# The first four contraction chunks of x and weights loaded one by one, at the start of a decoder layer

## The chip, the cores and the metric

The kernel runs on one core of one Trainium2 chip. The metric is the device time of one execution in microseconds (us), lower is better; a kernel's time is the median of its runs. A profile is one further execution, recorded by the hardware profiler. The engines are TensorE (PE, with its weight loads PEld), VectorE (DVE), ScalarE (ACT), GpSimd (POOL) and SyncE (SP), which only issues loads and stores.

## The reference

One decoder layer for 320 rows: a prompt of 256 and 8 samples of 8. D is 2048, float32 everywhere.

```python
xn = rms_norm(x, g_mix)
z = xn @ w_in                     # B, C, h, q, k, v, gate_conv, gate_attn
u = c_gate * h_conv
y_conv = (b_gate * short_conv(u)) @ w_conv_out
y_attn = window_attention(q, k, v, rel_bias, sinks) @ w_attn_out
m = sigmoid(gate_c) * y_conv + sigmoid(gate_a) * y_attn
h = x + m @ w_o
hn = rms_norm(h, g_ffn)
h = h + (silu(hn @ w_gate) * (hn @ w_up)) @ w_down
y = rms_norm(h, g_final)
```

The new keys and values and the convolution's last rows are outputs too.

## The kernel before

Activations lie with the features on the 128 partitions: x is 16 contraction chunks (KC) of 128 features by 320 rows (T). One chunk of x is 128 x 320 float32, 160 KB. The weights come as float32, too, and every product is made from high and low parts: a raw weight tile `wraw` is cast to `whi` on ScalarE (the cast rounds it to the matmul's input format), DVE subtracts to get the rest, `wlo`, and x is split into `xh_t` and `xl_t` in the same way. Three matmuls are then made for each chunk and column block: high by high, high weights by low x, low weights by high x.

The change touches the first product, the one for keys and values (`kv_product`). Its weights `w_kv` are 512 columns wide, so one chunk is 256 KB and takes 4 column blocks x 3 = 12 matmuls. A list of tile sizes (`tiles`) says how many chunks one weight load brings: 1, 1 and then seven times 2. `load_kv` issues a load, takes a tile for each part, and issues cast and subtraction; raw tiles have four buffers, the parts three each, so that a later load on the SP queue waits for the subtraction that frees its buffer. The first load goes out on ScalarE's queue, all others on SP's.

x comes through the tensor `xv`, whose first 72 columns (VW) are four small vectors (`g_mix`, `g_ffn`, the convolution's weights `wcv`, `g_fin`). It is loaded in pieces of `XB` chunks by `x_load`; the argument `x_after` says behind which weight load each piece is issued on SP. `x_prep` splits a chunk of x: the high part on ScalarE (chunk 0 on DVE), the low part on DVE. Inside the product it is called for the chunks of the next weight tile, behind one of the current tile's matmuls. `tick` takes the next step of `start_rest`: the squares for the norm, and the small loads on POOL, held by `gate` until chunk 3 of x is split.

The order on each engine is that in which the scheduler of the tile framework puts the instructions of the program; it is fixed when the kernel is built, and each engine then works in order.

Ahead of the product PE runs 20 matmuls on a constant tile `busy` (`wm`, L269), whose output is not used; DVE fills the tile first. `first_root` is a square root on ScalarE whose output is not used either; it makes the engine load that function's table.

Of the kernel before, what the change touches and what calls it, by code (L numbers as in the profile page):

```python
# [8 lines left out]
F32 = mybir.dt.float32  # L9
F32R = mybir.dt.float32r  # L10
AF = mybir.ActivationFunctionType
# [6 lines left out]
T = TP + NB * TS  # L18
# [8 lines left out]
P = 128  # L27
KC = D // P
CW = 256
# [2 lines left out]
O_GC = O_Q + NH * HD  # L32
O_GA = O_GC + D
EL = 384
LAG = 3
VW = 72
E0 = D - 512
TR = T - P
XB = [1, 1, 2, 2, 2, 2, 2, 4]
TOK = [(0, 128), (128, 128), (256, 64)]  # L40


# [1 line left out]
def hybrid_layer(ctx: ExitStack, tc: tile.TileContext, a: dict, o: list):  # L44
    nc = tc.nc
    y_0, y_r, nk_p, nv_p, nk_s, nv_s, ncv = o

    w_in, w_kv, w_co, w_ao, w_o, w_g, w_u, w_d = (
        a[n] for n in ("w_in", "w_kv", "w_conv_out", "w_attn_out", "w_o", "w_gate", "w_up", "w_down")
    )  # L50

    cst = ctx.enter_context(tc.tile_pool(name="cst", bufs=1))
# [10 lines left out]
    def ps_aux(name):  # L63
        return aux[0].tile([P, 512], F32, tag="aux", name=name)
# [3 lines left out]
    def u(s):  # L68
        uid[0] += 1
        return f"{s}_{uid[0]}"  # L70

    def after(*marks):

        es = ExitStack()
        for m in marks:
            es.enter_context(tc.issue_after(m.ins))
        return es
# [15 lines left out]
    def split_to(hi, lo, src):  # L93
        last["hi"] = nc.scalar.activation(hi, src, AF.Copy)  # L94
        last["lo"] = nc.vector.tensor_sub(lo, src, hi.bitcast(F32))  # L95
# [12 lines left out]
    last = {}  # L108
# [6 lines left out]
    def passes(order, end):  # L115

        seq, low = [], []
        for k, c in order:
# [3 lines left out]
            low.append((k, c, 2))  # L122
            if len(low) > LAG:
                seq.append(low.pop(0))
# [43 lines left out]


    ident = cst.tile([P, P], F32, name="ident")  # L170
    busy = cst.tile([P, CW], mybir.dt.bfloat16, name="busy")
    busy_in = nc.vector.memset(busy, 1.0)
    ones = cst.tile([P, 1], F32, name="ones")
    ones_r = cst.tile([P, P], F32R, name="ones_r")
    with after(busy_in):
        nc.vector.memset(ones, 1.0)
        nc.vector.tensor_copy(ones_r, ones.to_broadcast([P, P]))
    st_sb = cst.tile([P, 8, 2 * NB], F32, name="st_sb")
    sink_bc = cst.tile([P, NH], F32, name="sink_bc")
    nsink = cst.tile([P, NH], F32, name="nsink")  # L180
# [36 lines left out]
    xp = ctx.enter_context(tc.tile_pool(name="xp", bufs=1))  # L217
    xh_t = xp.tile([P, KC, T], F32R, tag="xh", name="xh_t")
    xl_t = xp.tile([P, KC, T], F32R, tag="xl", name="xl_t")

    xv = xp.tile([P, VW + KC * T], F32, name="xv")
    g_mix, g_ffn, wcv, g_fin = xv[:, 0:16], xv[:, 16:32], xv[:, 32:56], xv[:, 56:VW]
    hT = xv[:, VW:].rearrange("p (k t) -> p k t", k=KC)
    e_scr = dr.tile([NH, EL], F32, name="e_scr")

    def xh(kc):
# [18 lines left out]
    oh_r = zz.tile([NBK, WIN], F32R, name="oh_r")  # L245
    e_sb = zz.tile([NH, EL], F32, name="e_sb")

# [2 lines left out]
    st = sp.enter_context(tc.tile_pool(name="st", bufs=1))  # L250

    def x_load(i):
        c0, c1 = (VW + sum(XB[:j]) * T if j else 0 for j in (i, i + 1))
        nc.sync.dma_start(xv[:, c0:c1], a["x_v"][:, c0:c1])

    x_load(0)
    x_load(1)

    first_root = st.tile([P, 1], F32, name="first_root")
    nc.scalar.activation(first_root, ones, AF.Sqrt)  # L260
    nc.gpsimd.memset(ident, 0.0)
    nc.gpsimd.affine_select(
        out=ident, in_=ident, compare_op=ALU.not_equal, fill=1.0, base=0, pattern=[[-1, P]],
# [1 line left out]
    )  # L265

    wm = ps_aux("wm")
    for n in [CW] * 13 + [P] * 7:
        nc.tensor.matmul(wm[:, :n], busy[:, :P], busy[:, :n], start=True, stop=True)  # L269

    def x_prep(kc):
        if kc == 0:
            m1 = nc.vector.tensor_scalar(xh_t[:, kc, :], hT[:, kc, :], g_mix[:, kc:kc + 1], None, op0=ALU.mult)
        else:
            m1 = nc.scalar.activation(xh_t[:, kc, :], hT[:, kc, :], AF.Copy, scale=g_mix[:, kc:kc + 1])
        m2 = nc.vector.scalar_tensor_tensor(
            xl_t[:, kc, :], hT[:, kc, :], g_mix[:, kc:kc + 1], xh_t[:, kc, :].bitcast(F32),
            op0=ALU.mult, op1=ALU.subtract,
        )
        mark[kc] = (m1, m2)  # L280

    CK = 2 * DKV

    def load_kv(k0, n):
        raw = wp.tile([P, KT // 2, CK], F32, tag="wraw", name=u("wraw"), bufs=4)
        (nc.scalar if k0 == 0 else nc.sync).dma_start(raw[:, :n, :], w_kv[0, :, k0:k0 + n, :])
        hi = wp.tile([P, KT // 2, CK], F32R, tag="whi", name=u("whi"), bufs=3)
        lo = wp.tile([P, KT // 2, CK], F32R, tag="wlo", name=u("wlo"), bufs=3)
        with after(*mark[k0]):
            if k0 == 0:  # L290
                nc.scalar.activation(hi[:, 0, :CW], raw[:, 0, :CW], AF.Copy)
                last["hi"] = nc.scalar.activation(hi[:, 0, CW:], raw[:, 0, CW:], AF.Copy)
                last["lo"] = nc.vector.tensor_sub(lo[:, 0, :], raw[:, 0, :], hi[:, 0, :].bitcast(F32))
            else:
                split_to(hi[:, :n, :], lo[:, :n, :], raw[:, :n, :])
        return hi, lo

    def kv_product(tiles, x_after):

        ps = [ps_acc(u("kv")) for _ in range(4)]  # L300
        k0 = 0
        x_prep(0)
        for i, n in enumerate(tiles):
            hi, lo = load_kv(k0, n)
            if i == 0:
                x_prep(1)
            for b in x_after.get(i, ()):
                x_load(b)
            order = [(k, c) for k in range(n) for c in range(4)]
            if k0 + n == KC:  # L310
                order.sort(key=lambda kc: kc[1])
            seq = passes(order, k0 + n == KC)
            if i == 0:
                seq.sort(key=lambda kcm: kcm[2])
            for k, c, m in seq:
                kc = k0 + k
                if k0 and (k, c, m) == (0, 3 if n > 1 else 1, 0) and k0 + n < KC:
                    x_prep(k0 + n)
                    x_prep(k0 + n + 1)
                    tick()  # L320
                w, x = ((hi, xh), (hi, xl), (lo, xh))[m]
                last["mm"] = nc.tensor.matmul(  # L322
                    ps[c][:, :T], w[:, k, c * P:(c + 1) * P], x(kc),
                    start=(kc == 0 and m == 0), stop=(kc == KC - 1 and m == 2),
                )
            k0 += n
            if i == 0:
                tick()
        return ps
# [4 lines left out]
    def small_loads():  # L334

        behind = nc.gpsimd.tensor_copy(gate, xh_t[:, 3, 0:1].bitcast(F32))
        with after(behind):
            nc.gpsimd.dma_start(rel, a["rel_bias"])
            nc.gpsimd.dma_start(oh, a["c_onehot"])
            nc.gpsimd.dma_start(sink_bc, sk[0].partition_broadcast(P))  # L340
            nc.gpsimd.dma_start(sink_s, bass.AP(sk.tensor, sk.offset, [[1, NH], [0, TS], [1, 1]]))
            nc.gpsimd.dma_start(st_sb, a["state_t"])
            nc.gpsimd.dma_start(blk, a["c_block"])

    def squares(*chunks):

        for k in chunks:
            t = tmp("t" + "abcd"[k % 4], "sq")[:, :T] if k else xacc
            nc.scalar.activation(t, hT[:, k, :], AF.Square)
            if k:  # L350
                nc.vector.tensor_add(xacc, xacc, t)

    def start_rest():
        squares(0)
        yield
        small_loads()
        squares(1)
        for k in range(2, 12, 2):
            yield
            squares(k, k + 1)  # L360

    side_work[0] = start_rest()
    ps_kv = kv_product([1, 1] + [2] * 7, {1: (2,), 2: (3,), 3: (4,), 4: (5, 6), 5: (7,)})
    for _ in side_work[0]:
        pass
    for c in range(2):
# [11 lines left out]
    def first_norm():  # L378
# [15 lines left out]
        for z in (vT, kT):  # L394
# [5 lines left out]
        nc.gpsimd.dma_start(  # L400
            bias_s, bass.AP(e_scr.tensor, e_scr.offset + WIN - TS, [[EL, NH], [1, TS], [1, WIN + TS]])
        )
# [56 lines left out]
    def bias_load(kv, gp):  # L459
# [3 lines left out]
            bass.AP(  # L463
                e_scr.tensor, e_scr.offset + (kv * GRP + gp * 2) * EL, [[1, P], [EL, 2], [1, 2 * WIN]]
            ),
# [260 lines left out]
    for cp in range(4):  # L726
        c_sb = []
        ps = in_pair(O_C + cp * CW, "C")
        for c in range(2):
            t = tmp("ta", "csb")  # L730
# [4 lines left out]
        for c in range(2):  # L735
# [13 lines left out]
            n = UL - 2  # L749
# [11 lines left out]
        for c in range(2):  # L761
            ch = cp * 2 + c
            cv, cs = conv[c]
            t = tmp("td", "bc")
# [24 lines left out]
    for mp in range(8):  # L789
        c0 = mp * CW  # L790
        sg = {}
        for nm, off, tag in (("gc", O_GC, "ta"), ("ga", O_GA, "tb")):
            ps = in_pair(off + c0, nm)
            for c in range(2):
                t = tmp(tag, nm)[:, :T]
# [12 lines left out]
        for c in range(2):  # L808
            t = sg["ga", c]
# [11 lines left out]
    for mp in range(8):  # L821
        c0 = mp * CW
# [4 lines left out]
        for c in range(2):  # L827
            k = mp * 2 + c
# [8 lines left out]
            else:  # L837
                t = tmp("tc", "sq")[:, :T]
# [66 lines left out]
    for half in range(2):  # L905
# [5 lines left out]
        for fpair in range(nf // 2):  # L911
            c0 = (f0 + fpair * 2) * P
# [9 lines left out]
            for c in range(2):  # L922
                t, t2 = tmp("ta", "gs")[:, :T], tmp("tb", "sg")[:, :T]
# [76 lines left out]
    for j in range(nf // 2):  # L1000
        raw = wp.tile([P, 2, 512], F32, tag="wraw", name=u("wraw"), bufs=4)
        nc.sync.dma_start(raw, w_d[E0 // 512, :, FH[0] + 2 * j:FH[0] + 2 * j + 2, :])
        if j < 5:
            src, n = (free, 2 * j) if j < 3 else (more, 2 * (j - 3))
            hi, lo = (
                src[:, i * KT * CW:(i + 1) * KT * CW].rearrange("p (k n) -> p k n", k=2) for i in (n, n + 1)
            )
        else:
            hi = wp.tile([P, 2, 512], F32R, tag="whi", name=u("whi"), bufs=3)
# [28 lines left out]
    for c in range(4):  # L1038
        k = E0 // P + c
# [12 lines left out]
    for c in (2, 3):  # L1052
        k = E0 // P + c
# [126 lines left out]
```

## Time and profile before

| | |
|---|---|
| runs | 1678.95, 1676.19, 1676.61 us; median 1676.61 |
| profiled execution | 1676.44 us, its span 1674.5 us |
| mean granted TensorE clock | 0.998 |
| TensorE busy | 1664.1 us, 99% |
| DVE busy | 893.3 us, 53% |
| ACT busy | 651.1 us, 39% |
| read from HBM | 253.30 MB, 154 GB/s over the span |

The span goes from the first to the last recorded instruction; the rest of the execution's time lies around it. The rows of a timeline give start and duration in us, engine, line, operation, what is written and read, how many instructions were merged, and in brackets how long the engine was idle before and what ended that. In a table of stages the columns are the stage, its length, the busy time of PE, PEld, DVE, ACT and POOL with instruction counts, the granted clock, the DMA engines' mean busy share, and GB/s. Matmuls overlap: a duration is longer than the distance to the next start.

### The profile page before, as it was taken

Reading aid. Unit: us, or ns where it says so; the run is one execution under the profiler, and the core shown is the slowest. Engines: PE = TensorE matmul, PEld = TensorE weight load, DVE = VectorE, ACT = ScalarE, POOL = GpSimd, SP = SyncE. Lnnn points to the kernel's source line nnn. Section 1 sums busy time; section 2 is a strip of 40 time slices with the busy share of each in tenths; the row PEclk is TensorE's granted clock in tenths of the full one; section 3 lists DMA queues with packets and bytes.
Section 4 is the critical chain, followed back from the end, with each engine's and each line's share of the span. In section 5 each row is a group of like instructions: output and inputs, shape, how many; then the busy total and the mean of one; then the engine's idle time right before and its main releaser. Section 6 shows DMA issues by size and latency. Waiting matters only on the chain.

```text
span 1674.5 us, 26375 instructions
## 1 busy us (share of the span) xinstructions
PE 1664.1 (99%) x10983; PEld 1621.4 (97%) x10983; DVE 893.3 (53%) x1298; ACT 651.1 (39%) x863; POOL 79.5 (5%) x120
## 2 busy tenths in 40 slices
PE   9999999999999999999999999999999999999997
PEld 9999999999999999999999999998888999999887
DVE  7779554444444445556555555553444455555556
ACT  6445433333333333334333333333333333334443
POOL 0111311000000002320000000000000000000000
PEclk9999999999999999999999999999999999999999
DMA  7554546544444444444444444445555444444552
GB/s 257 169 153 140 177 138 185 160 150 150 150 152 151 151 149 150 148 149 149 151 151 151 151 150 148 148 149 151 150 151 151 151 151 151 151 151 149 175 167 89
DMA packets 73391, 258.13 MB, mean 154 GB/s; under 512 B 8440, under 2 KB 10920, under 8 KB 73144
## 3 DMA queue, kind: packets, MB, share of 16 engines
q1 hardware_dynamic: 71160, 250.28, 48.2%
q0 software_dynamic: 1968, 5.90, 1.3%
q8 instruction: 86, 1.41, 0.3%
q14 instruction: 33, 0.27, 0.0%
q10 hardware_dynamic: 144, 0.26, 0.0%
HBM read 253.30 MB, written 5.08 MB: 154 GB/s over the span
## 4 chain that ended last, share of the span: by engine, by line
PE 99%; DVE 0%; DMA 0%; SPq 0%; ACT 0%; issue 0%; DVEq 0%
PE fg L141 18%; PE fu L141 18%; PE dn L879 9%; PE ga L141 7%; PE wo L141 7%; PE gc L141 7%; PE dn L887 6%; PE B L141 3%; PE q L141 3%; PE C L141 3%; PE yc L141 3%; PE H L141 3%; PE ya L141 3%; PE dl L883 2%; PE kv L322 1%; PE dn L1026 1%
## 5 line engine op out<-in xcount | busy, mean ns | idle before, releaser
L95 DVE TENSOR_TENSOR wlo<-wraw,whi 128x1024 fp32r<-128x1024 f32 (+1 forms) x459 | 561.5, 1224 | 637.1 <-ACT whi L94 629.4
L94 ACT ACTIVATE whi<-wraw 128x1024 fp32r<-128x1024 f32 (+1 forms) x459 | 485.5, 1059 | 779.8 <-PE dn L879 157.7
L879 PE MATMUL dn<-a_t,whi 128*128 128x512 f32 x640 | 218.8, 394 | 0.0
L141 PE MATMUL fg<-hh_t,whi 128*128 128x320 f32 x704 | 212.4, 309 | 0.0
L141 PE MATMUL fu<-hh_t,whi 128*128 128x320 f32 x704 | 212.4, 309 | 0.0
L141 PE MATMUL fg<-hl_t,whi 128*128 128x320 f32 x704 | 212.3, 309 | 0.0
L141 PE MATMUL fu<-hl_t,whi 128*128 128x320 f32 x704 | 212.3, 309 | 0.0
L141 PE MATMUL fg<-hh_t,wlo 128*128 128x320 f32 x704 | 164.0, 309 | 0.0
L141 PE MATMUL fu<-hh_t,wlo 128*128 128x320 f32 x704 | 164.0, 309 | 0.0
L887 PE MATMUL dn<-a_t,wlo 128*128 128x320 f32 x640 | 152.0, 309 | 0.0
L879 PEld LDWEIGHTS dn<-a_t,whi 128*128 128x128 f32 x640 | 119.2, 188 | 23.5
L141 PEld LDWEIGHTS fg<-hl_t,whi 128*128 128x128 f32 x704 | 132.1, 188 | 0.0
L141 PEld LDWEIGHTS fu<-hl_t,whi 128*128 128x128 f32 x704 | 132.1, 188 | 0.0
L141 PEld LDWEIGHTS fg<-hh_t,whi 128*128 128x128 f32 x704 | 132.1, 188 | 0.0
L141 PEld LDWEIGHTS fu<-hh_t,whi 128*128 128x128 f32 x704 | 132.1, 188 | 0.0
L887 PEld LDWEIGHTS dn<-a_t,wlo 128*128 128x128 f32 x640 | 112.4, 188 | 10.9
L141 PEld LDWEIGHTS fu<-hh_t,wlo 128*128 128x128 f32 x704 | 118.5, 188 | 0.0
L141 PEld LDWEIGHTS fg<-hh_t,wlo 128*128 128x128 f32 x704 | 118.5, 188 | 0.0
L141 PE MATMUL ga<-xh_t,whi 128*128 128x320 f32 x256 | 77.3, 310 | 0.0
L141 PE MATMUL gc<-xh_t,whi 128*128 128x320 f32 x256 | 77.3, 310 | 0.0
L141 PE MATMUL ga<-xl_t,whi 128*128 128x320 f32 x256 | 77.3, 310 | 0.0
L141 PE MATMUL gc<-xl_t,whi 128*128 128x320 f32 x256 | 77.3, 310 | 0.0
(311 smaller groups left out, 2749.1 us busy)
## 6 DMA issues: line engine op xcount, KB each, us to landing
wraw<-in_w_in_dram SPq DMA_DIRECT2D x128, 512.0 KB, 3.8
wraw<-in_w_gate_dram SPq DMA_DIRECT2D x88, 512.0 KB, 3.8
wraw<-in_w_up_dram SPq DMA_DIRECT2D x88, 512.0 KB, 3.8
wraw<-in_w_down_dram SPq DMA_DIRECT2D x88, 512.0 KB, 3.7
wraw<-in_w_o_dram SPq DMA_DIRECT2D x32, 512.0 KB, 3.8
wraw<-in_w_conv_out_dram SPq DMA_DIRECT2D x16, 512.0 KB, 3.7
wraw<-in_w_attn_out_dram SPq DMA_DIRECT2D x16, 512.0 KB, 3.7
wraw<-in_w_kv_dram SPq DMA_DIRECT2D x7, 512.0 KB, 7.6
```

The lines of the kernel that those rows point to most:

```text
L94: last["hi"] = nc.scalar.activation(hi, src, AF.Copy)
L95: last["lo"] = nc.vector.tensor_sub(lo, src, hi.bitcast(F32))
L141: last["mm"] = nc.tensor.matmul(ps[c][:, :T], w[:, k, c * P:(c + 1) * P], x(kc), start=(kc == 0 and i == 0), stop=(kc == nk - 1 and i == 2),)
L322: last["mm"] = nc.tensor.matmul(ps[c][:, :T], w[:, k, c * P:(c + 1) * P], x(kc), start=(kc == 0 and m == 0), stop=(kc == KC - 1 and m == 2),)
L879: nc.tensor.matmul(ps[c], parts[k][0][:, cs], a_t[:, k, 0:512], start=k == 0, stop=False)
L883: nc.tensor.matmul(low, a_t[:, k, 512:], parts[k][0], start=k == 0, stop=k == nf - 1 and c0 < E0)
L887: last["mm"] = nc.tensor.matmul(ps[c][:, :T], parts[k][1][:, cs], a_t[:, k, 0:T], start=False, stop=k == nf - 1)
L1026: nc.tensor.matmul(ps[c][:, P:512], held[k][0][:, cs], a_t[:, k, P:512], start=k == 0, stop=k == nf - 1)
```

## The change

The first four chunks of x and of the `w_kv` weights are loaded and split one by one: `tiles` becomes four times 1 and six times 2, `XB` 1, 1, 1, 1, 2, 2, 2, 2, 4, and the pieces 7 and 8 are both issued behind the weight load of tile 5. The very first weight load becomes two, of 256 columns each, and its cast three, of 128, 128 and 256 columns. The square root on ScalarE is issued behind these loads. Of the small vectors only `g_mix` stays ahead of x; the others move to the end of the tensor and come with its last piece, and `xv` keeps its size. The warm-up reads a bf16 constant that the preamble has written, in place of `busy`, and has 15 matmuls of 256 columns and 7 of 128 instead of 13 and 7.

```diff
+VX = 16 + KC * T
-VW = 72
+VW = 16
-XB = [1, 1, 2, 2, 2, 2, 2, 4]
+XB = [1, 1, 1, 1, 2, 2, 2, 2, 4]
...
-    busy = cst.tile([P, CW], mybir.dt.bfloat16, name="busy")
-    busy_in = nc.vector.memset(busy, 1.0)
     ones = cst.tile([P, 1], F32, name="ones")
     ones_r = cst.tile([P, P], F32R, name="ones_r")
-    with after(busy_in):
-        nc.vector.memset(ones, 1.0)
-        nc.vector.tensor_copy(ones_r, ones.to_broadcast([P, P]))
+    nc.vector.memset(ones, 1.0)
+    nc.vector.tensor_copy(ones_r, ones.to_broadcast([P, P]))
...
-    xv = xp.tile([P, VW + KC * T], F32, name="xv")
-    g_mix, g_ffn, wcv, g_fin = xv[:, 0:16], xv[:, 16:32], xv[:, 32:56], xv[:, 56:VW]
-    hT = xv[:, VW:].rearrange("p (k t) -> p k t", k=KC)
+    xv = xp.tile([P, VX + 56], F32, name="xv")
+    g_mix, g_ffn, wcv, g_fin = xv[:, 0:VW], xv[:, VX:VX + 16], xv[:, VX + 16:VX + 40], xv[:, VX + 40:]
+    hT = xv[:, VW:VX].rearrange("p (k t) -> p k t", k=KC)
...
     def x_load(i):
-        c0, c1 = (VW + sum(XB[:j]) * T if j else 0 for j in (i, i + 1))
+        c0, c1 = (VW + sum(XB[:j]) * T if 0 < j < len(XB) else j and VX + 56 for j in (i, i + 1))
         nc.sync.dma_start(xv[:, c0:c1], a["x_v"][:, c0:c1])
...
-    nc.scalar.activation(first_root, ones, AF.Sqrt)
...
     wm = ps_aux("wm")
-    for n in [CW] * 13 + [P] * 7:
-        nc.tensor.matmul(wm[:, :n], busy[:, :P], busy[:, :n], start=True, stop=True)
+    one = lambda n: nc.const_aps.tensor(1.0, [P, n], mybir.dt.bfloat16)
+    for n in [CW] * 15 + [P] * 7:
+        nc.tensor.matmul(wm[:, :n], one(P), one(n), start=True, stop=True)
...
     def load_kv(k0, n):
         raw = wp.tile([P, KT // 2, CK], F32, tag="wraw", name=u("wraw"), bufs=4)
-        (nc.scalar if k0 == 0 else nc.sync).dma_start(raw[:, :n, :], w_kv[0, :, k0:k0 + n, :])
+        if k0 == 0:
+            for c0 in (0, CW):
+                behind = nc.scalar.dma_start(raw[:, 0, c0:c0 + CW], w_kv[0, :, 0, c0:c0 + CW])
+
+            with after(behind):
+                nc.scalar.activation(first_root, ones, AF.Sqrt)
+        else:
+            nc.sync.dma_start(raw[:, :n, :], w_kv[0, :, k0:k0 + n, :])
...
             if k0 == 0:
-                nc.scalar.activation(hi[:, 0, :CW], raw[:, 0, :CW], AF.Copy)
-                last["hi"] = nc.scalar.activation(hi[:, 0, CW:], raw[:, 0, CW:], AF.Copy)
+                for c0, c1 in ((0, P), (P, CW), (CW, CK)):
+                    last["hi"] = nc.scalar.activation(hi[:, 0, c0:c1], raw[:, 0, c0:c1], AF.Copy)
...
                 if k0 and (k, c, m) == (0, 3 if n > 1 else 1, 0) and k0 + n < KC:
-                    x_prep(k0 + n)
-                    x_prep(k0 + n + 1)
+                    for kk in range(tiles[i + 1]):
+                        x_prep(k0 + n + kk)
                     tick()
...
     def start_rest():
         squares(0)
         yield
+        squares(1)
+        yield
         small_loads()
-        squares(1)
-        for k in range(2, 12, 2):
+        squares(2)
+        yield
+        squares(3)
+        for k in range(4, 12, 2):
             yield
             squares(k, k + 1)
...
-    ps_kv = kv_product([1, 1] + [2] * 7, {1: (2,), 2: (3,), 3: (4,), 4: (5, 6), 5: (7,)})
+    ps_kv = kv_product([1] * 4 + [2] * 6, {1: (2,), 2: (3,), 3: (4,), 4: (5, 6), 5: (7, 8)})
...
-    inputs["x_v"] = _np.concatenate([vec.T, by_feature(x).reshape(P, -1)], axis=1)
+    inputs["x_v"] = _np.concatenate([vec.T[:, :16], by_feature(x).reshape(P, -1), vec.T[:, 16:]], axis=1)
```

In the changed kernel, the instructions stand on the two queues in this order, from the end of the single chunks to the weights of chunks 8 and 9:

```
SP:   weights 4,5 | x 6,7 | x 8,9 | weights 6,7 | x 10,11 | x 12 to 15 and vectors | weights 8,9
ACT:  cast weights 6,7 | squares 6, 7 | x splits 10, 11 | x splits 12, 13, 14, 15 | cast weights 8,9
```

In the kernel before, the weights of chunks 8 and 9 stand behind x 10,11 and ahead of x 12 to 15 on both.

## Prediction

> **What bounds the kernel now.** I read the page first, then the chain of waits over the first 40 us, the timeline of the start, the landing times of the single loads, and the page's queues last. The page says that TensorE (PE) is the bound nearly throughout.
>
> ```profile
> span 1674.5 us, 26375 instructions
> ## 1 busy us (share of the span) xinstructions
> PE 1664.1 (99%) x10983; PEld 1621.4 (97%) x10983; DVE 893.3 (53%) x1298; ACT 651.1 (39%) x863; POOL 79.5 (5%) x120
> ```
>
> PE is not busy for 1674.5 - 1664.1 = 10.4 us in all. No edit in the first stage can be worth more than that, and every edit here acts in the first stage. After it PE runs on without a break, so a microsecond won or lost at the start arrives at the end whole. The profiled execution took 1676.44 us, 1.94 us more than its span and 0.17 us below the median of the three runs (1676.61); I work against the profiled one. Here is what holds the start (chain of waits, first 40 us; start, duration, what):
>
> ```profile
> 2.60 6.13 DMA wraw<-in_w_kv_dram
> ...
> 8.76 1.07 ACT whi L94
> ...
> 9.87 25.08 PE kv L322 x168
> 34.95 5.13 PE q L141 x35
> ```
>
> The third weight load, a pair of contraction chunks (2 and 3), lands at 8.73; ScalarE needs 1.07 us to cast it; then PE works without a break until the next product. So before 9.87 transfers set the pace, and from there PE does. The timeline shows how the first product begins:
>
> ```profile
> 0.86 0.27 DVE L172 MEMSET busy<- 128x256 bf16 x1 [0.86 <-PEq L1163]
> ...
> 1.18 1.28 ACT L260 ACT_TABLE_LOAD   x1 [1.18 <-PEq L1163]
> ...
> 1.19 3.70 PE L269 MATMUL wm<-busy 128*128 128x256 bf16 x20 [1.19 <-DVE ones L176]
> ...
> 2.47 0.20 ACT L260 ACTIVATE first_root<-ones 128x1 f32<-128x1 f32 x1
> ...
> 3.73 1.17 PE L269 MATMUL wm<-busy 128*128 128x256 bf16 x8
> 4.34 0.39 DVE L273 TENSOR_SCALAR xh_t<-xv 128x320 fp32r<-128x320 f32 x1 [2.92 <-DMA xv<-in_x_v_dram]
> 4.53 0.42 ACT L291 ACTIVATE whi<-wraw 128x256 fp32r<-128x256 f32 x1 [1.85 <-DMA wraw<-in_w_kv_dram]
> ...
> 4.99 1.43 PE L322 MATMUL kv<-xh_t,whi 128*128 128x320 f32 x4
> 6.22 0.82 PE L322 MATMUL kv<-xl_t,whi 128*128 128x320 f32 x4
> 6.89 0.75 PE L322 MATMUL kv<-xh_t,wlo 128*128 128x320 f32 x4
> ...
> 8.65 0.75 PE L322 MATMUL kv<-xh_t,wlo 128*128 128x320 f32 x4
> 9.87 0.41 PE L322 MATMUL kv<-xh_t,whi 128*128 128x320 f32 x1 [0.47 <-ACT whi L94]
> 10.12 0.31 PE L322 MATMUL kv<-xl_t,whi 128*128 128x320 f32 x1
> ```
>
> Three losses are to be seen. The first real matmul waits until 4.99 for data. The first four then take 6.22 - 4.99 = 1.23 us, 0.31 us apart; later the pace is 25.08 us / 168 = 0.149 us from start to start. And there is a hole at 9.87. All three are what the change aims at. What it may disturb comes later: weights are loaded in the order of the SP queue, and the ones for chunks 8 and 9 arrive late and are cast shortly before PE reaches them.
>
> ```profile
> 7.56 0.40 SPq L286 DMA_DIRECT2D wraw<-in_w_kv_dram  x1
> 8.75 0.33 SPq L254 DMA_DIRECT2D xv<-in_x_v_dram  x1
> wraw<-in_w_kv_dram SPq DMA_DIRECT2D x1, 512.0 KB, 11.5
> xv<-in_x_v_dram SPq DMA_DIRECT2D x1, 640.0 KB, 11.7
> 17.57 1.02 ACT L275 ACTIVATE xh_t<-xv 128x320 fp32r<-128x320 f32 x2 [0.96 <-DMA xv<-in_x_v_dram]
> 19.13 1.06 ACT L94 ACTIVATE whi<-wraw 128x1024 fp32r<-128x1024 f32 x1 [0.55 <-DMA wraw<-in_w_kv_dram]
> 20.82 1.91 ACT L275 ACTIVATE xh_t<-xv 128x320 fp32r<-128x320 f32 x4
> 20.62 0.31 PE L322 MATMUL kv<-xh_t,whi 128*128 128x320 f32 x1
> ```
>
> The first two rows are issues on SP, the next two the same loads with their size and time from issue to landing. Weights 8 and 9 land at 7.56 + 11.5 = 19.06, x chunks 12 to 15 at 8.75 + 11.7 = 20.45. ScalarE was waiting both for x chunks 10 and 11 (17.57) and for these weights (19.13). Their cast ends at 20.19 and PE starts on them at 20.62: a margin of 0.43 us, and nobody saw it because PE was late itself. Why loads need 11 us is seen in the stages:
>
> ```profile
> 3.00:5.00 2.00, 1.90 (x14) 1.33 (x12) 0.62 (x2) 0.47 (x2) 0.00 (x0) 1.00 1.09 397
> 14.25:15.75 1.50, 1.50 (x12) 1.50 (x11) 1.50 (x4) 1.50 (x4) 0.00 (x0) 1.00 0.29 99
> ```
>
> The last two columns are the DMA engines' busy share and GB/s. The queue moves 397 GB/s when it flows, and for 1.5 us it moves 99, with over a megabyte issued and not landed.
>
> **The change, part by part.** *Warm-up.* PE no longer waits for DVE's 0.27 us memset and two short instructions behind it, so it begins between 0.75 (the first issues on SP stand at 0.74) and 0.86 (DVE's first instruction); I take 0.83. Before, twelve 256-column matmuls took 3.73 - 1.19 = 2.54 us, 0.212 each. Fifteen of them are 3.18 us, and seven of half the width 0.74: the warm-up is through at 0.83 + 3.92 = 4.75, 0.24 before today's first real matmul.
>
> *First data.* The first weights come in two halves of 128 KB; at 397 GB/s the first half is complete up to 0.33 us sooner, or no sooner if the halves land together. The first cast has 128 columns; it lies between the one-column instruction (0.20) and the 256-column one (0.42), so about 0.31, 0.11 less. The first x load is 28 KB smaller, 0.07 us: DVE's first split ends at about 4.66 instead of 4.73. The cast would be done at 4.53 - 0.33 + 0.31 = 4.51 in the best case and 4.84 in the worst. The first real matmul is due between 4.75 and 4.9, and I take 4.75, 0.24 earlier. Two more small steps hide: the table load moves behind a second DMA issue on ScalarE (0.4 us), and ends at about 3.1 with its square root, well before the weights land; DVE's other instructions start 0.3 us earlier, and nobody waits for them.
>
> *Slow pace at the start.* If the pace changes at 6.22 as before, the 0.24 us are run at half speed and yield 0.11 us; if it changes as much earlier as PE starts earlier (0.36 us), matmuls that took 0.31 take 0.149 for that long, together some 0.3 us. I take 0.2.
>
> [...]
>
> *Chunks 2 and 3 one by one.* Chunk 2 needs its own 256 KB, not the pair's 512 KB, and a 512-column cast instead of 1024. In queue order, 1256 KB stand up to its weights instead of 1700 KB up to the pair's; 444 KB less at 397 GB/s is 1.1 us, so about 7.6, and the cast is done before 8.5, ahead of PE, which finishes chunk 1 at about 9.0. The hole goes: the last four matmuls before it began at 8.65 and would have ended at 9.24, the second matmul behind it began at 10.12 instead of 9.39, so 0.73 us. Chunk 3 is due on PE 1.8 us later and has its weights by then. ScalarE and DVE each issue one more weight split; both are ahead of PE here.
>
> Up to here PE gains 0.2 + 0.73 = 0.93 us, and would be ready for chunks 8 and 9 at 20.62 - 0.93 = 19.69.
>
> *The order behind it.* This is the part that costs. The old kernel queues x chunks 10 and 11, then weights 8 and 9, then x chunks 12 to 15. The new one issues the x loads 7 and 8 (chunks 10 and 11; chunks 12 to 15 with the late vectors) together, before weights 8 and 9: 640 KB and 28 KB moved ahead, less the 28 KB taken from the first load. The ScalarE program goes along with it: all six splits of x chunks 10 to 15 now stand before the cast of weights 8 and 9, and ScalarE works in order. The same bytes up to the end of the pair have landed at 20.45 in the trace. Spread between 17.57 (chunks 10 and 11) and 20.45, the 640 KB of 1152 KB are there at 17.57 + 2.88 x 640/1152 = 19.17. Then four splits (1.91) until 21.08, the weights have to be there (20.45), and the cast (1.06) ends at 22.14. PE starts on chunk 8 at about 22.2 instead of 19.69: a new hole of 2.5 us, behind which the second half of the first product, every later product and the x-low splits of DVE are queued. Against today's 20.62 that is +1.6 us. The next casts find their data: weights 10 and 11, at 21.7 at the latest by the same spacing, are wanted 3.5 us after 22.2.
>
> The bounds: if the queue flowed at 397 GB/s from 3 us on, 4644 KB would be in at 15.0 and the cast through before 19.7, no hole, -0.9 us. If only the pause at 14.25 were gone (three quarters of 1.5 us), the cast would end at 21.0, +0.5. If the pause fell worse by as much, +2.7. I take the trace as it is, since the small loads on POOL and the bytes ahead of them are nearly the same: **+1.6 us**, 1676.44 + 1.6 = 1678.0, and from the median 1678.2.
>
> **The rivals.** *Faster.* The transfers arrive in time and the start's gain stays whole: -0.9, about 1675.6. For it: single loads and the earlier start of PE spread the work more evenly, and a pause seen in one execution may be shorter. Against it: it needs both the pause and the long lag behind it gone, since the cast must be ready 2.5 us earlier than worked out.
>
> [...]
>
> *It does nothing that counts.* The halves land together, PE's earlier start only lengthens the warm-up, and a small hole at chunk 8 eats the removed one: within 0.3 us, 1676.6.
>
> **How the numbers follow.** The forecast hole, of whatever size between +0.3 and +3, has 0.6; the gain kept, 0.2; the slow clock, 0.12; nothing, 0.08. The range takes the first two cases and leaves out most of the third: 1675.4 to 1679.9. A measurement of this kernel tells 0.2% from no change, 3.35 us. The likeliest case, the gain and the zero all lie within that; beyond it on the slow side lie the slow clock and the top of the forecast hole, 0.15; on the fast side almost nothing can, as the start has under 2 us to give: 0.02. Same: 0.83.
>
> **What would show it.** In the changed profile the warm-up should start near 0.83 and the first real matmul near 4.75; no hole at chunk 2; PE idle for 2 to 3 us at about 20, released by the cast of weights 8 and 9, with ScalarE's four splits of x directly before it. If PE runs from 4.75 to the end of the first product unbroken, the queue argument is wrong. If the idle time is there but sits before another chunk, the spacing of landings is wrong. A first product that ends earlier than 33.9 or later than 38 contradicts the sum.

## The result

The changed kernel is slower: 1679.55 us, the median of 22 runs (1677.42 to 1681.54), against 1676.42 of the old one in 22 runs. The ratio is 1.0017, 95% interval [1.0012, 1.0023], and the difference 3.13 us. The forecast was a slower kernel at 1678.2, with a range up to 1679.9.

The profiled execution of the changed kernel took 1681.54 us, the longest of its runs, over a span of 1679.7 us; the mean granted clock is 0.996 where the old one had 0.998. PE is busy for 3.1 us more, though it has nothing more to compute than two warm-up matmuls (page, first part):

```profile
span 1679.7 us, 26390 instructions
PE 1667.2 (99%) x10985; PEld 1624.1 (97%) x10985; DVE 893.3 (53%) x1298; ACT 651.3 (39%) x865; POOL 79.6 (5%) x120
```

The chain of waits over the first 45 us names a new bound: the last piece of x, issued at 8.7 us, then the four splits of it on ScalarE, then the cast of weights 8 and 9, then PE.

```profile
8.72 11.56 DMA xv<-in_x_v_dram
...
20.31 1.12 ACT xh_t L273 x3
...
21.68 0.55 ACT xh_t L273
22.23 0.95 ACT whi L95
...
23.23 17.11 PE kv L327 x96
```

PE's timeline shows the start and the new holes, and then something else:

```profile
0.78 4.11 PE L267 MATMUL wm<-const-bfloat16-1.0 128*128 128x256 bf16 x22 [0.78 <-PEq L1172]
4.64 1.25 PE L327 MATMUL kv<-xh_t,whi 128*128 128x320 f32 x4
...
6.32 0.75 PE L327 MATMUL kv<-xh_t,wlo 128*128 128x320 f32 x4
...
8.08 0.75 PE L327 MATMUL kv<-xh_t,wlo 128*128 128x320 f32 x4
...
9.84 0.75 PE L327 MATMUL kv<-xh_t,wlo 128*128 128x320 f32 x4
...
11.60 0.75 PE L327 MATMUL kv<-xh_t,wlo 128*128 128x320 f32 x4
13.01 0.42 PE L327 MATMUL kv<-xh_t,whi 128*128 128x320 f32 x1 [0.66 <-ACT whi L95]
...
19.92 0.75 PE L327 MATMUL kv<-xh_t,wlo 128*128 128x320 f32 x4
23.23 0.63 PE L327 MATMUL kv<-xh_t,whi 128*128 128x320 f32 x1 [2.56 <-ACT whi L95]
23.66 0.47 PE L327 MATMUL kv<-xl_t,whi 128*128 128x320 f32 x1
23.93 0.47 PE L327 MATMUL kv<-xh_t,whi 128*128 128x320 f32 x1
24.19 0.47 PE L327 MATMUL kv<-xl_t,whi 128*128 128x320 f32 x1
```

The hole of the old kernel at chunk 2 is gone: from 6.32 to 11.60 the groups of four low-weight matmuls follow each other every 1.76 us. Chunk 4 has a new hole of 0.66 us. At chunk 8 PE waits for 2.56 us. Behind that, matmuls come every 0.267 us (23.66, 23.93, 24.19) instead of every 0.147. The stages show why, and show the pause of the transfers again (last three columns: granted clock, DMA share, GB/s):

```profile
14.50:16.00 1.50, 1.50 (x12) 1.50 (x12) 1.50 (x5) 1.50 (x4) 0.00 (x0) 1.00 0.28 76
22.25:22.50 0.25, 0.00 (x0) 0.00 (x0) 0.25 (x2) 0.25 (x1) 0.00 (x0) 1.00 0.20 82
22.50:22.75 0.25, 0.00 (x0) 0.00 (x0) 0.25 (x1) 0.25 (x1) 0.00 (x0) 0.64 0.16 66
22.75:29.25 6.50, 6.02 (x22) 6.02 (x23) 5.29 (x8) 4.04 (x8) 0.00 (x0) 0.50 0.52 144
```

The granted clock falls to a half while PE idles and stays there for 6.5 us. The first product gives way to the next one at 40.18 us in the changed kernel (q, first matmul) and at 34.78 in the old one:

```profile
40.18 0.31 PE L142 MATMUL q<-xh_t,whi 128*128 128x320 f32 x1
```

```profile
34.78 0.31 PE L141 MATMUL q<-xh_t,whi 128*128 128x320 f32 x1
```

That is 5.40 us. Up to chunk 8 it is 23.23 - 20.62 = 2.61; the rest, 2.79, is the halved clock: from chunk 8 to the end of the product it takes 16.95 us, and took 14.16 before. The spans differ by 5.2. So this one execution paid more than the median's 3.13. How much of the median is hole and how much is clock, the experiments have to tell.

### The profile page after: what moved, and what is told of

The parts are those of the page before. It is cut to its first block, busy times and chain, and to the rows that moved or that the text cites. A ratio compares the mean times of both kernels' runs of the same rounds, so it can differ in the third digit from the quotient of the medians.

```text
span 1679.7 us, 26390 instructions
## 1 busy us (share of the span) xinstructions
PE 1667.2 (99%) x10985; PEld 1624.1 (97%) x10985; DVE 893.3 (53%) x1298; ACT 651.3 (39%) x865; POOL 79.6 (5%) x120
## 4 chain that ended last, share of the span: by engine, by line
PE 98%; DMA 1%; ACT 0%; DVE 0%; issue 0%; SPq 0%; ACTq 0%; DVEq 0%
PE fg L142 18%; PE fu L142 18%; PE dn L888 9%; PE ga L142 7%; PE wo L142 7%; PE gc L142 7%; PE dn L896 6%; PE B L142 3%; PE C L142 3%; PE q L142 3%; PE yc L142 3%; PE H L142 3%; PE ya L142 3%; PE dl L892 2%; PE kv L327 1%; DMA xv<-in_x_v_dram 1%
```

## Experiments

My theory is the queue order: x chunks 12 to 15 ahead of weights 8 and 9 make the hole, and the hole lets the clock fall. The rivals are that the four single tiles are at fault (four raw buffers hold four chunks instead of six), and that the transfers' pause, not the order, sets the time. Each kernel has 11 runs, with the old kernel beside them: at 1676.55 us beside the two orders, the filled hole and the first kernel with late small loads; at 1676.32, on another chip, beside the next four (order and late loads, old kernel with late loads, half filled hole, changed kernel again); at 1676.39 beside the last four.

**The order, put back in the changed kernel and moved in the old one.**

```diff
 # changed kernel, order back
-    {1: (2,), 2: (3,), 3: (4,), 4: (5, 6), 5: (7, 8)}
+    {1: (2,), 2: (3,), 3: (4,), 4: (5, 6), 5: (7,), 6: (8,)}
 # old kernel, order moved
-    {1: (2,), 2: (3,), 3: (4,), 4: (5, 6), 5: (7,)}
+    {1: (2,), 2: (3,), 3: (4,), 4: (5, 6, 7)}
```

> The changed kernel, with the x piece of chunks 12 to 15 issued behind the weights of chunks 8 and 9 again instead of ahead of them. If the queue order makes the hole at chunk 8: the cast of weights 8 and 9 ends at about 20.2 as before, PE goes on at 20.5 without a hole, its clock stays full, and the time is about 1676.3 us, 3.2 below the changed kernel and level with the old one. If the four single tiles are at fault (four raw buffers hold four chunks instead of six, so later weights are issued later): hole and time stay, about 1679.5.

Measured: 1676.61 us, ratio to the old kernel 1.000 [0.9991, 1.0009]. The time came out as expected, but not the picture: there is still a hole at chunk 8 (this kernel's timeline of PE, then of ScalarE).

```profile
18.71 0.75 PE L327 MATMUL kv<-xh_t,wlo 128*128 128x320 f32 x4
20.53 0.41 PE L327 MATMUL kv<-xh_t,whi 128*128 128x320 f32 x1 [1.07 <-ACT whi L95]
```

```profile
19.42 1.06 ACT L95 ACTIVATE whi<-wraw 128x1024 fp32r<-128x1024 f32 x1 [2.70 <-DMA wraw<-in_w_kv_dram]
```

PE is there at 18.71 + 0.59 = 19.30, over a microsecond ahead of the old kernel, and has to wait for weights that land at 19.4 (19.06 in the old kernel). So the single tiles are not at fault: they are still there, and the loss is gone. With the transfers as they are, the order costs about 3 us, and without it the start's gain is still lost, to the transfers.

> The old kernel, with only the x piece of chunks 12 to 15 moved ahead of the weights of chunks 8 and 9. Queue order: the cast of weights 8 and 9 ends at 22.2 where PE is ready at 20.62, a hole of 1.6 us; 1678.0 if the clock stays full, up to 1680.6 if it halves behind the hole. Single tiles at fault: no loss, 1676.4.

Measured: 1677.68 us, ratio 1.0007 [0.9998, 1.0016]; 1.13 us above the old kernel's median, where 1.6 was expected. The wait has two parts in its profile, 0.32 us at 21.26 for the cast and then a late low part:

```profile
21.26 0.41 PE L322 MATMUL kv<-xh_t,whi 128*128 128x320 f32 x1 [0.32 <-ACT whi L94]
...
22.85 0.41 PE L322 MATMUL kv<-xh_t,wlo 128*128 128x320 f32 x1
```

Eight matmuls at 0.147 us after 21.26 the low part was due at about 22.5; it came at 22.85, released by DVE's subtraction for the low weights, which began at 21.58 and took 1.23 us (chain of waits). The two stretches seldom cost the clock: its mean is 0.998 or 0.999 in ten of the runs and 0.997 in one, the longest (1678.85). The first product ends 1.07 us later than in the old kernel's profile (35.85 against 34.78); 0.15 of that had come about at chunk 2, and the rest lies at these two waits. So the order by itself, with the old tiles, makes the kernel slower by about a microsecond. The interval alone would not say so, since it takes in 1; the waits in the trace do.

**The hole filled, half filled, and left as it is.**

```diff
+            if k0 == 8:
+                fl = ps_aux("fl")
+                for _ in range(22):        # 11 in the half filled one
+                    with after(last["mm"]):
+                        last["mm"] = nc.tensor.matmul(fl[:, :CW], one(P), one(CW), start=True, stop=True)
```

> The changed kernel, with 22 unused 256-column matmuls on the constant between chunks 7 and 8 (2.4 us at full clock, as long as the hole). If the halved clock behind the hole is a part of the loss: the granted clock stays at 1.00 at 23 us, the 24 matmuls of chunks 8 and 9 keep a distance of 0.147 us instead of 0.267, and the time falls by up to 2.6 us to about 1677.3, near the fastest of the changed kernel's runs (1677.42). If the clock is no part of it, or if more work cannot hold it: 1679.5.

Measured: 1678.29 us (1677.13 to 1680.03), granted clock 0.998 or 0.999 in each of the 11 runs. Doing 22 useless matmuls made the kernel faster by 1.3 us against the changed kernel's 1679.55, by 1.8 against its 1680.08 below, which is from another chip. In its profile (timeline of PE) the clock holds at 1.00 and the matmuls of chunk 8 follow each other every 0.147 us:

```profile
19.14 2.64 PE L324 MATMUL fl<-const-bfloat16-1.0 128*128 128x256 bf16 x22
21.53 0.39 PE L332 MATMUL kv<-xh_t,whi 128*128 128x320 f32 x1
21.77 0.31 PE L332 MATMUL kv<-xl_t,whi 128*128 128x320 f32 x1
```

The gain is not the 2.6 us that the profiled execution of the changed kernel had suggested. In this profile the filler itself ends later than the cast (21.53 against 21.29), and the changed kernel, to judge by its times, does not lose the whole 2.8 us in each execution. Nor is the hole of one length: the cast of weights 8 and 9 starts at 22.14, 21.25, 20.25 and 21.52 in the profiles of the changed kernel, its repetition below, the filled and the half filled one, with the big loads in the same order in all four.

> The changed kernel with 11 unused 256-column matmuls in the hole at chunk 8 (1.2 us at its front) instead of none or 22. [...]

Measured: 1678.15 us, 1.9 below the changed kernel beside it (1680.08). Eight runs lie at 1677.19 to 1678.38 and three at 1679.79 to 1680.01, these with a mean clock of 0.997 or 0.998. In the profiled one PE idled for 1.78 us and the clock stayed at 1.00:

```profile
22.61 0.42 PE L332 MATMUL kv<-xh_t,whi 128*128 128x320 f32 x1 [1.78 <-ACT whi L95]
```

To judge by their times, three runs of eleven still lost the clock. How long PE idled in these three is not known, since only one execution is profiled; so the idle time from which the clock falls is not shown.

> The changed kernel as it is, beside the others on the same chip. 1679.5 us, with a mean granted clock of 0.996 to 0.998 over the runs where the filled holes have 0.998 to 0.999; runs in which the clock holds should lie near 1677.5 to 1678.3.

Measured: 1680.08 us (1678.03 to 1680.51), and a profiled execution that happened to keep its clock (PE timeline, then stages):

```profile
19.07 0.75 PE L327 MATMUL kv<-xh_t,wlo 128*128 128x320 f32 x4
22.34 0.41 PE L327 MATMUL kv<-xh_t,whi 128*128 128x320 f32 x1 [2.52 <-ACT whi L95]
22.60 0.31 PE L327 MATMUL kv<-xl_t,whi 128*128 128x320 f32 x1
22.74 0.31 PE L327 MATMUL kv<-xh_t,whi 128*128 128x320 f32 x1
```

```profile
20.00:22.25 2.25, 0.00 (x0) 0.00 (x0) 1.94 (x4) 2.25 (x5) 0.00 (x0) 1.00 0.91 371
22.25:25.00 2.75, 2.65 (x17) 2.58 (x18) 2.57 (x4) 2.75 (x7) 0.00 (x0) 1.00 0.35 97
```

The same hole, 2.52 us, a clock of 1.00 throughout, matmuls 0.147 us apart behind it, and a span of 1676.1 us, 1.6 above the old kernel's. This pair of profiles of one and the same kernel separates hole from clock: with the hole alone it is 1.6 us slower, in the other one 5.2. Of the 3.6 us between them 0.9 come from the later start of chunk 8 (23.23 against 22.34), and the rest, 2.7, from the clock's fall. This kernel's two fastest runs, 1678.03 and 1678.34, are the two with a mean clock of 0.999. The other nine have 0.997 or 0.998 and 1679.12 to 1680.51.

**The small loads on POOL.** The gate and the call are moved so that the six loads wait for chunk 15 of x, in the changed kernel, in the one with the order put back, and in the old kernel.

```diff
-        behind = nc.gpsimd.tensor_copy(gate, xh_t[:, 3, 0:1].bitcast(F32))
+        behind = nc.gpsimd.tensor_copy(gate, xh_t[:, 15, 0:1].bitcast(F32))
...
     def start_rest():
...
-        small_loads()
...
         for k in range(4, 12, 2):
             yield
             squares(k, k + 1)
+        yield
+        small_loads()
```

> The changed kernel, with POOL's six small loads held until chunk 15 of x is split (about 22 us) instead of chunk 3. If these loads make the queue pause at 14.5 to 16 us: the pause goes from there, x chunks 12 to 15 land 1 to 1.5 us sooner, the hole at chunk 8 shrinks from 2.6 to about 1.3 us, the clock holds, about 1677 us. If the pause has another cause: pause, hole and time stay, 1679.5; late small loads could cost something near 30 us, where the first of them is read.

Measured: 1676.16 us (1675.54 to 1676.61), 0.9996 [0.9987, 1.0004] of the old kernel. Moving six small loads takes back the whole loss, though the order of the big loads is still the changed one. ScalarE no longer waits for x: its six splits of chunks 10 to 15 run in one piece, the cast of weights 8 and 9 follows (timeline), and PE's waits are short (list of its waits: total, count, longest).

```profile
16.03 2.81 ACT L273 ACTIVATE xh_t<-xv 128x320 fp32r<-128x320 f32 x6
18.75 1.04 ACT L95 ACTIVATE whi<-wraw 128x1024 fp32r<-128x1024 f32 x1
```

```profile
PE kv L327 <- DVE wlo L96: 0.4, 1, 0.4
PE kv L327 <- ACT whi L297: 0.3, 1, 0.3
PE kv L327 <- ACT whi L95: 0.2, 1, 0.2
```

> The changed kernel with both: x chunks 12 to 15 behind the weights of chunks 8 and 9 again, and POOL's small loads held until chunk 15 is split. If the start's gain is real and only the queue took it back: the chain reaches chunk 8 at about 19.5 and finds its weights cast, no hole beyond 0.3 us, 1675.4 us, 1.1 below the old kernel. If something else is the next to be late (weights 4 and 5, or DVE's splits of low parts): 1676 or above, with a hole that names it.

Measured: 1674.95 us (1674.53 to 1675.48), 0.9989 [0.9980, 0.9998] of the old kernel. There is no hole at chunk 8 any more (list of PE's waits), and the pause is gone (stage; 0.28 and 76 GB/s in the changed kernel):

```profile
PE wm L267 <- PEq L1173: 0.8, 1, 0.8
PE kv L327 <- ACT whi L297: 0.6, 1, 0.6
PE rowacc L1074 <- ACT jk L960: 0.6, 1, 0.6
```

```profile
14.50:16.00 1.50, 1.50 (x12) 1.50 (x11) 1.50 (x5) 1.50 (x4) 0.00 (x0) 1.00 1.04 429
```

> The old kernel with POOL's small loads held until chunk 15 is split. In its profile no hole lies behind the pause at 14.25, only a margin of 0.43 us: the median should stay at 1676.4 within 0.4, and the single runs near 1679, if they come from a longer pause, should be gone. If the pause costs the old kernel in most runs, the median falls by 0.5 us or more.

Measured: 1676.50 us (1676.03 to 1677.24), 0.9999 [0.9990, 1.0008]. Its stage at 14.25 to 15.75 shows the transfers flowing, and yet nothing is won:

```profile
14.25:15.75 1.50, 1.50 (x12) 1.50 (x11) 1.50 (x4) 1.50 (x4) 0.00 (x0) 1.00 1.03 417
```

So the pause lay just inside the old kernel's margin; the changed kernel, which arrives a microsecond earlier and asks for more bytes first, runs into it. None of these 11 runs comes near 1679, but only 4 of the 33 runs of the old kernel beside them did, so this alone does not show that the pause makes those. All kernels with late small loads together point that way: none of their 77 runs lies more than 1.1 us above its kernel's median, while 11 of the 99 runs of the old kernel beside the experiments lie more than 2 us above theirs.

**What of the start is worth something.** Three kernels each take one part back from the kernel with order and late loads, and that kernel runs again beside them.

```diff
 # old warm-up
-    for n in [CW] * 15 + [P] * 7:
-        nc.tensor.matmul(wm[:, :n], one(P), one(n), start=True, stop=True)
+    for n in [CW] * 13 + [P] * 7:          # with busy, its memset and after(busy_in)
+        nc.tensor.matmul(wm[:, :n], busy[:, :P], busy[:, :n], start=True, stop=True)
 # one first load
-            for c0 in (0, CW):
-                behind = nc.scalar.dma_start(raw[:, 0, c0:c0 + CW], w_kv[0, :, 0, c0:c0 + CW])
+            behind = nc.scalar.dma_start(raw[:, :n, :], w_kv[0, :, k0:k0 + n, :])
-                for c0, c1 in ((0, P), (P, CW), (CW, CK)):
+                for c0, c1 in ((0, CW), (CW, CK)):
 # pairs: the old XB, tiles, x_after and start_rest
-XB = [1, 1, 1, 1, 2, 2, 2, 2, 4]
+XB = [1, 1, 2, 2, 2, 2, 2, 4]
```

> The kernel with order and late small loads, and with the old warm-up (the tile that DVE fills, 13 wide matmuls). If the warm-up's earlier start is worth the 0.2 us that the prediction gave it: the first real matmul moves from 4.2 to 4.6 back to about 4.9, the fast pace comes about 0.4 us later, 1675.2 against 1674.95. If it is worth nothing: 1674.95.

> The kernel with order and late small loads, and with the first weights in one load and two casts again. If the halves bring the first matmul forward: it stands at about 4.9 and the time is 1675.2. If PE waits for the second half anyway (0.59 us of idle time after the second matmul in the profile of the kernel with both): the same time, 1674.95.

> The kernel with order and late small loads, and with the old tile sizes (chunks 2 and 3 in one load). If single chunks are what wins: a hole of 0.2 to 0.7 us at chunk 2 comes back, and with it 0.5 to 0.9 us, 1675.4 to 1675.9. If the gain comes from warm-up and halves: no more than 1675.1.

> The kernel with order and late small loads once more, as the control of the three beside it: 1674.95 within 0.3.

Measured, with the old kernel at 1676.39 beside them:

| kernel | median us | runs | ratio to the old kernel |
|---|---|---|---|
| order and late loads, again | 1675.09 | 1674.38 to 1676.11 | 0.9989 [0.9980, 0.9997] |
| with the old warm-up | 1675.03 | 1674.42 to 1675.51 | 0.9990 [0.9981, 1.0000] |
| with one first load | 1674.60 | 1674.37 to 1675.24 | 0.9988 [0.9979, 0.9997] |
| with pairs | 1676.27 | 1675.56 to 1677.06 | 0.9996 [0.9988, 1.0005] |

The single chunks carry the gain: with pairs 1.2 us are lost, more than the 0.5 to 0.9 expected, and PE waits for chunk 2 again, for longer than the 0.2 to 0.7 us expected (this kernel's list of PE's waits):

```profile
PE kv L327 <- ACT whi L95: 1.2, 1, 1.2
```

The warm-up makes no difference that these runs show; with the old one the first real matmul stands at 4.65, not at the 4.9 expected. Nor do the halves help; the kernel without them is the fastest median of all, 0.5 us below that of the kernel with halves, though the two ranges overlap and the order of these two stays open. It starts the first product later and ends it earlier than the kernel with the old warm-up, whose first matmuls run slowly (first matmuls and first matmul of the next product, of the one-load kernel and then of the old warm-up):

```profile
4.79 0.87 PE L326 MATMUL kv<-xh_t,whi 128*128 128x320 f32 x4 [0.28 <-ACT whi L296]
5.50 0.75 PE L326 MATMUL kv<-xl_t,whi 128*128 128x320 f32 x4
...
33.07 0.31 PE L142 MATMUL q<-xh_t,whi 128*128 128x320 f32 x1
```

```profile
4.65 1.56 PE L329 MATMUL kv<-xh_t,whi 128*128 128x320 f32 x4
6.01 0.90 PE L329 MATMUL kv<-xl_t,whi 128*128 128x320 f32 x4
...
34.09 0.31 PE L142 MATMUL q<-xh_t,whi 128*128 128x320 f32 x1
```

When the fast pace begins differs between executions of kernels with the same warm-up: the second group of four matmuls takes 0.59 us from start to start in the one-load kernel's profile and 0.90 in that of the kernel with order and late loads, run again. So the end of the first product in one profile says little about halves or warm-up.

## Why the prediction was right, and where it was off

*The start.* PE was forecast to begin at 0.83 and did at 0.78; the first real matmul at 4.75, seen at 4.64 and 4.37 in the two profiles. The hole at chunk 2 was forecast to go, and went. PE was to be ready for chunk 8 at 19.69; in the second profile it was, at 19.07 + 0.59 = 19.66. The term "0.2 us from the earlier start" is not confirmed: without the new warm-up or without the halves the time is the same or lower. The gain of about 1 us is that of the single chunks: 1.2 with the later loads out of the way, where 0.73 was forecast for the hole at chunk 2.

*Chunk 4* I passed over with "chunk 3 has its weights by then", and did not price the next tile. Weights 4 and 5 were late in the first profile, 0.66 us, and cost nothing at the end, since chunk 8 waits longer whenever PE gets there.

*The order behind it* is the step that decided, and it came out as worked: the cast forecast to end at 22.14, PE on chunk 8 at 22.2; seen 22.34 in one profile and 23.23 in the other. There x chunks 12 to 15 landed at 20.29, a microsecond later than the 19.17 spaced out of the old trace. Of "+1.6 us" the profile with a steady clock shows 1.6 in the span. That it fits so closely is partly luck, since with the same order of loads the cast started anywhere from 20.25 to 22.14 in four profiles. And the order makes the hole only together with the pause: without the pause, with the order still changed, PE waits 0.2 and 0.4 us there.

*The mis-sized step is the clock.* I gave a slow clock behind the hole 0.12, as if the 2.5 us that I had worked out were too short for it; from what length of a hole the clock falls, no run shows. Its price was 2.8 us in the profile in which it fell. To judge by their times, the clock fell in most executions: 20 of the 22 runs and nine of the 11 beside the experiments lie above 1679. Forecast hole and slow clock were not two cases but one with a lottery in it. The median, 1679.55, is about 1.3 us above that of the filled kernels (1678.29 and 1678.15); that this is the clock is shown by filling the hole, which takes 1.3 to 1.9 us back. Why it is not the whole 2.8 that one profile shows stays open, since no profile caught such an execution.

*Luck in the range.* The measured 1679.55 lies 0.35 us inside it. The prediction had no case of a hole with a part of the clock's price, and the same kernel's median in the later runs, 1680.08, lies outside. The prediction's own sign is crossed, too: it said that a first product that ends later than 38 contradicts the sum. The next product starts at 40.18 in the profile where the clock fell, and at 36.61 where it held; the sum had no term for the clock. The prediction also took 3.35 us for the least difference that a measurement can tell; 22 runs of each kernel told 3.13.

*The bounds.* "If only the pause were gone, +0.5" was tried: 1676.16, 0.4 below the old kernel. That bound had the cast end at 21.0; it ended at 19.79, because ScalarE had x chunks 12 to 15 without a wait: its splits of chunks 10 to 15 ran in one piece from 16.03, where in the changed kernel's profile, with 11.6 us from issue to landing, those of 12 to 15 began at 20.31, after 2.25 us of idle time. I had taken only three quarters of the pause off their landing, 1.1 us.

*The rival "faster"* asked for the pause and the lag to be gone. With the small loads late and the order put back the cast is in time, and the start's gain stands: 1.4 us below the old kernel, where the rival had 0.9.

## What to carry to other kernels

When an edit lets the bounding engine arrive earlier, look for the next transfer that had been just in time: its margin in the old trace (here 0.43 us) is all that the edit can win there, and an order of loads that was harmless becomes a stall (here 2.56 and 2.52 us of idle PE in the changed kernel's two profiles). Issue weights before data that are needed later than they, in the queue and in the order of the casts both, and keep small loads of another queue away from the stretch in which the big ones are awaited (76 GB/s from 14.5 to 16 us in the changed kernel, 429 with order put back and late small loads). Price a stall on TensorE at its length and the chance that the clock falls behind it (here 1.6 us of span with the clock held, 5.2 with it fallen).

## What the runs showed of the hardware that I had not expected

The clock: in one execution it was still granted in full 1.8 us into an idle stretch of 2.56 us and was at 0.50 from 2.1 us on, for 6.5 us, of which PE worked 6.0; and it stayed at 1.00 through an idle stretch of 2.52 us in another execution of the same kernel. So a length of the hole from which it decides cannot be given. Unused work in the hole made the fall rarer, to judge by times and clocks: the mean clock is 0.998 or 0.999 in all 11 runs with the filled hole, and 0.997 or 0.998 in nine of the changed kernel's 11 runs beside the experiments.

The slow pace at the start does not stand in the column of the granted clock: it is 1.00 from 5 to 6.25 us in the old kernel's profile, where the matmuls follow each other every 0.31 us instead of 0.149. That both slow paces have one cause is therefore not shown by these profiles.

Six small loads on POOL, 92.5 KB together, all but stop the big transfers for some 1.5 us, beginning about 6 us after the first of them is issued and 3 after the last. From 14.5 to 16 us the seven profiles with early small loads have 76 to 166 GB/s; with late ones the changed kernel has 410, the old one 420, and the one with the order put back 429. That these loads are the cause is shown by moving them; by what means they hold up the other queue is not. Held until chunk 15 is split, they cost PE no wait that the three profiles list.
